# A fourth buffer for x, two fewer for the gate's projections, and half of the low parts of x made by VectorE, at the head of a hybrid encoder kernel

## The chip, the cores and the metric

The kernel runs on one core of a Trainium2 chip. The metric is the time of one execution on the device, in microseconds (us); the time of a kernel is the median of its runs. Engines are named as in the profile: PE (TensorE matmul; PEld its weight loads), DVE (VectorE), ACT (ScalarE), POOL (GpSimd), SP (SyncE, which issues all DMA transfers here; SPq is its queue).

## The reference

A trunk of two layers on 512 tokens of width 1024, all in f32. Layer 0 mixes tokens by neighbourhood attention, layer 1 by latent attention. Each layer ends with a gated addition of a "per-layer embedding" (PLE): a sigmoid gate times p[i] @ ple_w_proj[i]. The change touches only the head of layer 0.

```python
def rmsnorm(x, g):
    y = x * lax.rsqrt(jnp.mean(x * x, axis=-1, keepdims=True) + EPS)
    return y * g
...
for i in range(DEPTH):                                   # DEPTH = 2
    xn = rmsnorm(x, norm_g[i])
    y = mixer_na(xn, ...) if i % 2 == 0 else mixer_mla(xn, ...)   # x @ w_in -> q, k, v, z; attention; * silu(z); @ w_out
    h = x + y
    gate = jax.nn.sigmoid(rmsnorm(h, ple_norm[i]) @ ple_w_gate[i])
    x = h + gate * (p[i] @ ple_w_proj[i])
return rmsnorm(x, final_norm)
```

## The kernel before, in words

Every matrix product is done as three: each operand is cut into a high part (ACT copies it into the float32r type) and a low part, its "rest" (f32 value minus high part, made by POOL or DVE), and PE adds high x high, high x low and low x high in PSUM. So each weight tile that SP loads into `wraw` gives a `whi` (ACT, L76) and a `wlo` (POOL, L77), and `wraw`, `whi` and `wlo` have three buffers each.

A scheduler in the framework sets the order of the instructions of each engine from the code and from its own timeline; the order is then fixed, and each engine works through its list strictly in turn. A `tile_pool` hands out buffers by tag: a tile waits until the last readers of the tile that held its buffer are done.

The head of the program, `run` in the "pre" pool, goes as follows.

1. x comes in twice. `xT` is x with features on the partitions, 8 tiles of 128x512. Times the gain g0 it is cut into `rh` (ACT, L629) and `rl` (DVE, L630): the pair `raw`, x not yet normalised. The second form, `x` (L642), has tokens on the partitions, 4 tiles of 128x1024; ACT squares each in place and sums the squares into a column of `ssq` (L643).
2. `ple` makes p[0] @ ple_w_proj[0] for 4 token tiles and 2 column halves (n = 0, 1). The 8 results go from PSUM to tiles called `pe` (DVE for n = 0, L415; ACT for n = 1, L417), and from there SP stores them to DRAM (L418).
3. POOL turns `ssq` into 1/rms (L645, L646); PE transposes it, spread over 128 columns, into `ps_T` (L122), so that each column holds the factor of its token. ACT copies that to `R` (L649).
4. The gate's input z of the mixer is projected from `raw`, and scaled by R only afterwards (`z_phase`): z0 and z1 with weights loaded ahead (L167), then z2, z3 and z4 (L96; their results are `ps_S`, `ps_S` and `ps_mm`). DVE multiplies each by R (L159), ACT applies SiLU (L160).
5. For each of the 8 tiles of `xT`, DVE multiplies by ps_T and g0 (L653), ACT copies the high part `xh` (L654), POOL makes the rest `xl` (L655). This pair is x normalised.
6. `na_heads` follows, in the "na" pool. Its first product is v of head group 0, from xh and xl: 4 token tiles of 24 matmuls of 128x256 each (8 with xh and whi, 8 with xl and whi, 8 with xh and wlo). Then q and k of the first two heads, and attention.

In the rows of the engines' order that are quoted below, names carry the number of their buffer: `rh_125`, `rh_126`, `rl_127`, `rl_128` are the two halves of `raw`; `xh_129`, `xh_130`, `xl_131`, `xl_132` those of normalised x; `pe_82` to `pe_85` are the tensors in DRAM that hold PLE's results.

Of the kernel before, what the change touches and what calls it, by code (L numbers as in the profile page):

```python
# [13 lines left out]
F32 = mybir.dt.float32  # L14
F32R = mybir.dt.float32r
AF = mybir.ActivationFunctionType
ALU = mybir.AluOpType
AX = mybir.AxisListType
PSUM = bass.MemoryType.PSUM
P = 128  # L20
S = 512
D = 1024
NT = S // P
# [15 lines left out]
class Trunk:  # L39
# [567 lines left out]
    def run(self):  # L607
        tc, nc, a = self.tc, self.nc, self.a
        def pair(n):
            return [self.bigtile(f"{n}h{g}") for g in range(2)], [self.bigtile(f"{n}l{g}") for g in range(2)]  # L610
# [4 lines left out]
        with tc.tile_pool(name="pre", bufs=4, reuse_waits="tile") as pool:  # L615
            operands = self.ple_load(0, pool)
            g0 = pool.tile([P, KD], F32, name="g0", bufs=1)
            nc.sync.dma_start(g0, a["g0"])

            raw, xT = pair("r"), pair("x")  # L620
            part = lambda T, k: [T[s][k // 4][:, k % 4, :] for s in range(2)]
            xs = [pool.tile([P, S], F32, name="xT", tag="xT", bufs=8) for k in range(KD)]
            ws = [[self.wp.tile([P, 1024], d, name=n, tag=n, bufs=3)
                   for n, d in (("wraw", F32), ("whi", F32R), ("wlo", F32R))] for _ in range(2)]
            for h in range(2):
                for k in range(4 * h, 4 * h + 4):
                    nc.sync.dma_start(xs[k], a["xT"][k])
                    hi, lo = part(raw, k)
                    nc.scalar.activation(hi, xs[k], AF.Copy, scale=g0[:, k:k + 1])  # L629
                    nc.vector.scalar_tensor_tensor(lo, xs[k], g0[:, k:k + 1], hi.bitcast(F32), op0=ALU.mult,  # L630
                                                   op1=ALU.subtract)
                for j in range(2):
                    wr, hi, lo = (x[:, h * S:(h + 1) * S] for x in ws[j])
                    nc.sync.dma_start(wr, a["na_z"][j][:, h * S:(h + 1) * S])
                    nc.scalar.activation(hi, wr, AF.Copy)
                    nc.vector.tensor_tensor(out=lo, in0=wr, in1=hi.bitcast(F32), op=ALU.subtract)
            ws = [w[1:] for w in ws]
            nc.sync.dma_start(self.ident, a["ident"])
            ss = pool.tile([P, NT], F32, name="ssq", bufs=1)
            xt = [pool.tile([P, D], F32, name="x", tag="x", bufs=3) for t in range(NT)]  # L640
            for t in range(NT):
                nc.sync.dma_start(xt[t], a["x"][t])  # L642
                nc.scalar.activation(xt[t], xt[t], AF.Square, accum_out=ss[:, t:t + 1])  # L643
            self.ple(pool, 0, "pe", 8, operands)
            nc.gpsimd.tensor_scalar(ss, ss, 1.0 / D, EPS, op0=ALU.mult, op1=ALU.add)  # L645
            nc.gpsimd.tensor_tensor(out=ss, in0=ss, in1=self.half.to_broadcast([P, NT]), op=ALU.pow)  # L646
            turned = self.transposes([ss[:, t:t + 1].to_broadcast([P, P]) for t in range(NT)])
            R = pool.tile([P, S], F32, name="R", bufs=1)
            nc.scalar.activation(R, turned, AF.Copy)  # L649
            zs = self.z_phase(a["na_z"], raw, range(2), R=R, ws=ws)  # L650
            for k in range(KD):
                hi, lo = part(xT, k)
                nc.vector.scalar_tensor_tensor(xs[k], turned, g0[:, k:k + 1], xs[k], op0=ALU.mult, op1=ALU.mult)  # L653
                nc.scalar.activation(hi, xs[k], AF.Copy)  # L654
                nc.gpsimd.tensor_tensor(out=lo, in0=xs[k], in1=hi.bitcast(F32), op=ALU.subtract)  # L655
            zs.update(self.z_phase(a["na_z"], raw, range(2, 8 - NLATE), R=R))
        oT = ([self.bigtile(f"oh{g}") for g in range(2)], [self.bigtile(f"ol{g}") for g in range(2)])
        with tc.tile_pool(name="na", bufs=2, reuse_waits="tile") as pool:
# [176 lines left out]
```

## Time and profile before

| | before |
|---|---|
| median of 3 runs | 691.34 us (691.29 to 692.84) |
| profiled execution: its time | 689.97 us |
| profiled execution: its span | 688.2 us |
| mean granted PE clock | 0.992 of full |
| PE busy | 664.4 us (97%) |
| ACT busy | 406.6 us (59%) |
| POOL busy | 397.8 us (58%) |
| DVE busy | 363.8 us (53%) |
| HBM traffic, mean over the span | 109 GB/s |

The span is the time from the first to the last record of the profiled execution; its own time is 1.8 us longer. Busy shares are averages over all stages. In the rows of the timeline the first number is the start in us from the start of the span, the second the time from there to the end of the group, then the engine, the line, the operation, output and inputs with their shapes and the count; in brackets stands how long the engine was idle before, and what ended that.

### The profile page before, as it was taken

The numbers are of one execution on the slowest core, as the hardware profiler recorded it, in microseconds if no ns is written. First come the engines' busy times: TensorE is split into PE (matmuls) and PEld (weight loads), VectorE is DVE, ScalarE is ACT, GpSimd is POOL, SyncE is SP. The second block draws the span as 40 slices with busy tenths as digits, with TensorE's granted clock in tenths as the row PEclk, the third lists the DMA queues.
The fourth block names the chain that finished last, engine by engine and source line by source line (L and its number), as shares of the span: only waits on it lengthen the run. The fifth ranks groups of instructions, "written<-read, shape, count | busy, mean of one in ns | idle before, by whom it ended". The sixth has DMA issues, their size and how long they took to land.

```text
span 688.2 us, 10108 instructions
## 1 busy us (share of the span) xinstructions
PE 664.4 (97%) x3552; PEld 566.3 (82%) x3552; DVE 363.8 (53%) x829; ACT 406.6 (59%) x808; POOL 397.8 (58%) x312
## 2 busy tenths in 40 slices
PE   7988999999999999999999998999999999999995
PEld 5878898998988888788899886787888777888885
DVE  6140374637837614633524503788988886045334
ACT  6662576666767562643533634878888878426433
POOL 0385457466575565853044634777789867658511
PEclk9998999999999999999999999999999999999998
DMA  8932423323223128444242343203121201584222
GB/s 281 375 112 72 133 81 104 104 74 108 73 93 115 35 104 306 153 130 135 92 114 95 106 118 119 80 24 92 25 69 37 87 1 65 190 311 153 62 74 95
DMA packets 30371, 79.11 MB, mean 115 GB/s; under 512 B 3953, under 2 KB 7281, under 8 KB 30321
## 3 DMA queue, kind: packets, MB, share of 16 engines
q1 hardware_dynamic: 30320, 78.47, 34.5%
q8 instruction: 28, 0.46, 0.3%
q14 instruction: 23, 0.18, 0.1%
HBM read 66.92 MB, written 8.39 MB: 109 GB/s over the span
## 4 chain that ended last, share of the span: by engine, by line
PE 85%; ACT 6%; DVE 3%; POOL 2%; issue 2%; DMA 2%; SPq 0%; POOLq 0%; DVEq 0%; ACTq 0%
PE ps_mm L96 59%; PE ps_S L96 10%; PE ps_T L122 5%; PE ps_O L96 4%; PE ps_O L357 2%; PE ps_mm L167 2%; PE ps_T L345 1%; ACT ex L596 1%; DMA wraw<-proj 1%; ACT whi L76 1%; PE ps_S L310 1%; PE ps_S L309 1%; POOL xl L655 1%; DVE mx L594 1%; POOL wlo L77 1%
## 5 line engine op out<-in xcount | busy, mean ns | idle before, releaser
L77 POOL TENSOR_TENSOR wlo<-wraw,whi 128x1024 fp32r<-128x1024 f32 (+3 forms) x93 | 210.4, 2275 | 131.4 <-ACT whi L76 97.2
L76 ACT ACTIVATE whi<-wraw 128x1024 fp32r<-128x1024 f32 (+3 forms) x93 | 92.0, 999 | 83.8 <-PE ps_mm L96 20.2
L598 POOL TENSOR_TENSOR ex<-ex,rc 128x512 f32<-128x512 f32 x64 | 66.2, 1046 | 20.8 <-DVE rc L597 14.0
L96 PE MATMUL ps_mm<-whi,hnT 128*128 128x512 f32 (+1 forms) x272 | 69.7, 377 | 0.0
L96 PEld LDWEIGHTS ps_mm<-whi,hnT 128*128 128x128 f32 x272 | 49.5, 188 | 9.5
L332 POOL TENSOR_TENSOR ex<-ex,rc 128x128 f32<-128x128 f32 (+1 forms) x64 | 34.3, 560 | 37.9 <-DVE rc L328 36.4
L594 DVE TENSOR_REDUCE mx<-ps_S 128x1 f32<-128x512 f32 x64 | 43.7, 685 | 15.3 <-PE ps_S L96 14.3
L596 ACT ACTIVATE ex<-ps_S,mx 128x512 f32<-128x512 f32 x64 | 44.0, 689 | 8.2 <-DVE mx L594 6.7
L85 DVE TENSOR_TENSOR pt_lo<-ps_T,pt_hi 128x512 fp32r<-128x512 f32 x64 | 43.1, 679 | 5.0 <-ACT pt_hi L83 4.6
L327 ACT ACTIVATE ex<-ex,mx 128x128 f32<-128x128 f32 (+1 forms) x64 | 30.2, 473 | 21.9 <-DVE mx L323 21.5
L83 ACT ACTIVATE pt_hi<-ps_T 128x512 fp32r<-128x512 f32 x64 | 37.1, 598 | 7.6 <-PE ps_T L122 7.3
L96 PE MATMUL ps_mm<-xh,whi 128*128 128x512 f32 x152 | 41.0, 400 | 0.1
L96 PE MATMUL ps_mm<-wlo,hnT 128*128 128x512 f32 (+1 forms) x136 | 40.6, 379 | 0.0
L96 PE MATMUL ps_mm<-xh,wlo 128*128 128x512 f32 x152 | 39.2, 392 | 0.0
L96 PE MATMUL ps_mm<-xl,whi 128*128 128x512 f32 x152 | 38.8, 392 | 0.0
L122 PE MATMUL ps_T<-ident,ex 128*128 128x128 f32 x256 | 36.3, 273 | 0.2 <-DVE pt_lo L85 0.2
L122 PEld LDWEIGHTS ps_T<-ident,ex 128*128 128x128 f32 x256 | 30.7, 140 | 6.8 <-issue 0.7
L437 DVE TENSOR_TENSOR sg<-pe,sg 128x512 f32<-128x512 f32 (+1 forms) x17 | 12.5, 734 | 39.4 <-ACT sg L436 39.4
L96 PEld LDWEIGHTS ps_mm<-xl,whi 128*128 128x128 f32 x152 | 28.1, 188 | 5.8
L96 PEld LDWEIGHTS ps_mm<-xh,wlo 128*128 128x128 f32 x152 | 28.1, 188 | 5.5
L190 POOL TENSOR_TENSOR u<-u,z 128x512 f32<-128x512 f32 x16 | 20.6, 1290 | 19.6 <-DVE u L185 18.8
L106 POOL TENSOR_TENSOR rs<-ss,half 128x1 f32<-128x1 f32 x20 | 10.8, 549 | 36.2 <-DVE ss L105 34.9
(267 smaller groups left out, 1670.1 us busy)
## 6 DMA issues: line engine op xcount, KB each, us to landing
pe<-pe SPq DMA_DIRECT2D x32, 256.0 KB, 3.3
wraw<-na_qk SPq DMA_DIRECT2D x16, 512.0 KB, 3.4
wraw<-gate SPq DMA_DIRECT2D x16, 512.0 KB, 3.3
wraw<-na_v SPq DMA_DIRECT2D x8, 512.0 KB, 3.4
wraw<-na_o SPq DMA_DIRECT2D x8, 512.0 KB, 3.4
wraw<-mla_z SPq DMA_DIRECT2D x8, 512.0 KB, 3.7
wraw<-mla_o SPq DMA_DIRECT2D x8, 512.0 KB, 3.5
wraw<-na_z SPq DMA_DIRECT2D x6, 512.0 KB, 6.3
```

Source lines behind the costliest of these rows:

```text
L76: nc.scalar.activation(hi[:, c], raw[:, c], AF.Copy)
L77: (rest or nc.gpsimd).tensor_tensor(out=lo[:, c], in0=raw[:, c], in1=hi[:, c].bitcast(F32), op=ALU.subtract)
L83: nc.scalar.activation(hi, src, AF.Copy, scale=scale)
L85: nc.vector.tensor_tensor(out=lo, in0=src, in1=hi.bitcast(F32), op=ALU.subtract)
L96: last = nc.tensor.matmul(out, l, r, start=i == 0, stop=i == n - 1)
L122: self.nc.tensor.transpose(t[:, i * P:(i + 1) * P], b, self.ident)
L190: nc.gpsimd.tensor_tensor(out=u, in0=u, in1=z, op=ALU.mult)
L327: self.last_exp = nc.scalar.activation(e, e, AF.Exp, bias=mx[:, qt:qt + 1], accum_out=sm[:, qt:qt + 1])
L332: nc.gpsimd.tensor_tensor(out=e, in0=e, in1=rc[:, qt:qt + 1].to_broadcast([P, e.shape[1]]), op=ALU.mult)
L594: nc.vector.reduce_max(mx[:, c], sp, axis=AX.X, negate=True)
L596: nc.scalar.activation(ex, sp, AF.Exp, bias=mx[:, c], accum_out=sm[:, c])
L598: nc.gpsimd.tensor_tensor(out=ex, in0=ex, in1=rc[:, c].to_broadcast([P, S]), op=ALU.mult)
```

## The change

Three edits, all in `run`'s "pre" pool. The token-major `x` gets four buffers in place of three, so that none of its four tiles shares a buffer. The tag `pe` gets six buffers in place of eight, so that the last two of the eight PLE results reuse those of the first two. (4 KB per partition more for x, 2 x 2 KB less for pe.) And of the eight rests `xl` of normalised x, those with an even number are made by DVE, those with an odd number by POOL as before.

```diff
-            xt = [pool.tile([P, D], F32, name="x", tag="x", bufs=3) for t in range(NT)]
+            xt = [pool.tile([P, D], F32, name="x", tag="x", bufs=4) for t in range(NT)]
             for t in range(NT):
                 nc.sync.dma_start(xt[t], a["x"][t])
                 nc.scalar.activation(xt[t], xt[t], AF.Square, accum_out=ss[:, t:t + 1])
-            self.ple(pool, 0, "pe", 8, operands)
+            self.ple(pool, 0, "pe", 6, operands)
...
                 nc.scalar.activation(hi, xs[k], AF.Copy)
-                nc.gpsimd.tensor_tensor(out=lo, in0=xs[k], in1=hi.bitcast(F32), op=ALU.subtract)
+                (nc.vector, nc.gpsimd)[k % 2].tensor_tensor(out=lo, in0=xs[k], in1=hi.bitcast(F32), op=ALU.subtract)
```

The scheduler orders the head anew; behind the products of v every engine's order is as before, but for one weight load and three loads of the bias that change places on SP. Three places show it.

On SP, where all loads and stores are issued, in the stretch with the four tiles of x, the stores of PLE's results and the weights of z2, z3 and z4:

```order
-L642 DMA x<-x 128x1024 x3
+L642 DMA x<-x 128x1024 x4
 L418 DMA pe_82<-pe 128x512
 L418 DMA pe_83<-pe 128x512
 L418 DMA pe_84<-pe 128x512
 L418 DMA pe_85<-pe 128x512
-L75 DMA wraw<-na_z 128x1024 x2
-L642 DMA x<-x 128x1024
+L75 DMA wraw<-na_z 128x1024 x3
 L418 DMA pe_82<-pe 128x512
 L418 DMA pe_83<-pe 128x512
-L75 DMA wraw<-na_z 128x1024
```

The last tile of x moves ahead of the first four stores and of the weights of z2 and z3, and the weights of z4 ahead of two stores. On ACT the squares of the last two tiles of x likewise come ahead of the copies of the last two PLE results (the two that now reuse a buffer) and of the high parts of z2 and z3.

On PE, from the start of z2 (`ps_S`, first of its two) to the transposes of 1/rms near the end of z3, before:

```order
L96 MATMUL ps_S<-rh_125,whi 128x512 x4
L96 MATMUL ps_S<-rh_126,whi 128x512 x4
L96 MATMUL ps_S<-rl_127,whi 128x512 x4
L96 MATMUL ps_S<-rl_128,whi 128x512 x4
L96 MATMUL ps_S<-rh_125,whi 128x512 x4
L96 MATMUL ps_S<-rh_126,whi 128x512 x3
L96 MATMUL ps_S<-rh_125,wlo 128x512 x4
L96 MATMUL ps_S<-rh_126,wlo 128x512 x4
L96 MATMUL ps_S<-rh_126,whi 128x512
L96 MATMUL ps_S<-rl_127,whi 128x512 x4
L96 MATMUL ps_S<-rl_128,whi 128x512 x3
L122 MATMUL ps_T<-ident,ssq 128x128 x4
```

And now, from the end of z0 and z1 (L167) on:

```order
L167 MATMUL ps_mm<-rl_128,whi 128x512 x2
L167 MATMUL ps_mm<-rh_126,wlo 128x512 x2
L122 MATMUL ps_T<-ident,ssq 128x128 x4
L96 MATMUL ps_S<-rh_125,whi 128x512 x4
L96 MATMUL ps_S<-rh_126,whi 128x512 x4
L96 MATMUL ps_S<-rl_127,whi 128x512 x4
```

The four transposes move 39 matmuls forward, to the place right behind z0 and z1. No matmul is added or dropped. In the first tile of v the eight matmuls with xl and the eight with wlo now follow each other, where before those of the second tile were mixed in between.

On POOL, from its first work to the last rest of x:

```order
-L77 ISA
-L77 TENSOR_TENSOR wlo<-wraw,whi 128x1024 x2
+L645 ISA
 L645 TENSOR_SCALAR ssq<-ssq 128x4
 L646 TENSOR_TENSOR ssq<-ssq,half 128x4
 L77 TENSOR_TENSOR wlo<-wraw,whi 128x1024 x3
-L655 TENSOR_TENSOR xl_131<-xT,xh_129 128x512 x4
-L655 TENSOR_TENSOR xl_132<-xT,xh_130 128x512
+L655 TENSOR_TENSOR xl_131<-xT,xh_129 128x512 x2
 L77 TENSOR_TENSOR wlo<-wraw,whi 128x1024
-L655 TENSOR_TENSOR xl_132<-xT,xh_130 128x512 x3
+L655 TENSOR_TENSOR xl_132<-xT,xh_130 128x512 x2
+L77 TENSOR_TENSOR wlo<-wraw,whi 128x1024 x2
```

1/rms (L645, L646) moves ahead of the rests of z2 and z3, and the rests of x ahead of those of v's second weight tile and q's. On DVE the four rests that it takes over follow the eight products of L653, three of them ahead of z2's product with R, the fourth behind it.

## The prediction

> **What bounds the kernel now.** I read the page's busy shares first, then the busy time of the stages, then PE's timeline at its longest pause, and from there the engines that it waits for.
>
> ```profile
> PE 664.4 (97%) x3552; PEld 566.3 (82%) x3552; DVE 363.8 (53%) x829; ACT 406.6 (59%) x808; POOL 397.8 (58%) x312
> 45.57:64.87 19.30, 15.32 (x97) 13.93 (x96) 2.94 (x6) 5.71 (x12) 11.64 (x11) 0.82 0.18 62
> 64.87:688.20 623.33, 608.42 (x3286) 519.57 (x3284) 339.97 (x789) 370.07 (x751) 370.12 (x288) 1.00 0.32 104
> ```
>
> PE is the bound: other engines matter only where PE waits for them. The second row is the stage in which v is projected (duration, then busy time of PE, PEld, DVE, ACT, POOL, then PE's granted clock, DMA share and GB/s): PE has pauses in it and a clock of 0.82. Behind it, 623.33 us pass at full clock with 608.42 us of matmuls.
>
> PE's timeline, with an earlier pause for comparison:
>
> ```profile
> 12.31 0.50 PE L96 MATMUL ps_T<-whi 128*128 128x512 f32 x1 [0.42 <-ACT whi L399]
> ...
> 28.32 0.62 PE L167 MATMUL ps_mm<-rh,wlo 128*128 128x512 f32 x2
> 28.78 1.98 PE L96 MATMUL ps_S<-rh,whi 128*128 128x512 f32 x8
> ...
> 37.62 0.60 PE L122 MATMUL ps_T<-ident,ssq 128*128 128x128 f32 x4
> 37.97 0.48 PE L96 MATMUL ps_S<-rl,whi 128*128 128x512 f32 x1
> ...
> 45.57 2.25 PE L96 MATMUL ps_mm<-whi,xh 128*128 128x256 f32 x8
> 47.65 0.52 PE L96 MATMUL ps_mm<-whi,xl 128*128 128x256 f32 x3
> ...
> 52.74 0.79 PE L96 MATMUL ps_mm<-whi,xl 128*128 128x256 f32 x2 [2.77 <-POOL xl L655]
> 53.96 0.79 PE L96 MATMUL ps_mm<-whi,xl 128*128 128x256 f32 x2 [0.43 <-POOL xl L655]
> 55.19 0.58 PE L96 MATMUL ps_mm<-whi,xl 128*128 128x256 f32 x1 [0.43 <-POOL xl L655]
> ...
> 59.12 1.11 PE L96 MATMUL ps_mm<-whi,xh 128*128 128x256 f32 x8
> 60.07 1.12 PE L96 MATMUL ps_mm<-whi,xl 128*128 128x256 f32 x8
> ...
> 64.87 2.00 PE L96 MATMUL ps_mm<-xh,whi 128*128 128x512 f32 x8
> ```
>
> The stage holds 4 x 24 = 96 matmuls of 128x256. From 59.12 to 60.07 eight take 0.96 us (0.12 each), so 96 need 11.52 us; they take 64.87 - 45.57 = 19.30. The excess is 7.78 us: 3.63 in three pauses for POOL's `xl`, 2.08 - 0.96 = 1.12 in the first eight (45.57 to 47.65), the remaining 3.03 because matmuls run slowly after the pauses. The clock is lost by a pause of 2.77 us and its followers; the 0.42 us at 12.31 lost none.
>
> Why is `xl` late? POOL, DVE and ACT, in that order:
>
> ```profile
> 32.66 0.19 POOL L645 TENSOR_SCALAR ssq<-ssq 128x4 f32<-128x4 f32 x1
> 32.94 1.02 POOL L646 TENSOR_TENSOR ssq<-ssq,half 128x4 f32<-128x4 f32 x1
> 33.93 4.75 POOL L77 TENSOR_TENSOR wlo<-wraw,whi 128x1024 fp32r<-128x1024 f32 x2
> ...
> 49.12 2.34 POOL L77 TENSOR_TENSOR wlo<-wraw,whi 128x1024 fp32r<-128x1024 f32 x1
> 51.43 3.71 POOL L655 TENSOR_TENSOR xl<-xT,xh 128x512 fp32r<-128x512 f32 x3
> 38.88 1.29 DVE L159 TENSOR_TENSOR z<-ps_mm,R 128x512 f32<-128x512 f32 x2 [18.40 <-ACT R L649]
> 40.09 5.35 DVE L653 SCALAR_TENSOR_TENSOR xT<-ps_T,g,xT 128x512 f32<-128x512 f32 x8
> 45.36 1.28 DVE L159 TENSOR_TENSOR z<-ps_S,R 128x512 f32<-128x512 f32 x2
> 19.64 1.06 ACT L643 ACTIVATE x<-x 128x1024 f32<-128x1024 f32 x1 [0.83 <-DMA x<-x]
> 21.64 1.07 ACT L643 ACTIVATE x<-x 128x1024 f32<-128x1024 f32 x1
> 23.63 1.09 ACT L643 ACTIVATE x<-x 128x1024 f32<-128x1024 f32 x1
> 26.69 1.06 ACT L76 ACTIVATE whi<-wraw 128x1024 fp32r<-128x1024 f32 x1 [1.89 <-DMA wraw<-na_z]
> 28.01 1.06 ACT L76 ACTIVATE whi<-wraw 128x1024 fp32r<-128x1024 f32 x1 [0.26 <-DMA wraw<-na_z]
> 29.81 1.06 ACT L643 ACTIVATE x<-x 128x1024 f32<-128x1024 f32 x1 [0.74 <-DMA x<-x]
> 39.81 1.28 ACT L160 ACT_TABLE_LOAD   x1
> 42.17 2.70 ACT L654 ACTIVATE xh<-xT 128x512 fp32r<-128x512 f32 x5
> ```
>
> The fourth tile of x lands at 29.81, so 1/rms is done at 33.93, is transposed at 37.62, and DVE can normalise only from 40.09 to 45.36. POOL then makes eight rests of 1.24 us (3 in 3.71), with a weight rest in between, until 55.14. DVE has nothing to do meanwhile.
>
> **The change, part by part.**
>
> *Fourth buffer for x.* The weights of z2 and z3 land 26.69 and 28.01: 512 KB cost 1.32 us in the queue. The third tile had landed when ACT took it (23.63, no wait), so the fourth, now right behind it, lands by 24.95. ACT's squares follow at a pitch of 1.05 to 1.15, so the last ends at 26.1 at the latest, and POOL's two steps (32.66 to 33.93: 1.27) end by 27.4. PE comes to the transposes at 28.78: no wait, 1.4 us in hand. The transposes themselves cost 0.35 (37.62 to 37.97) in either place.
>
> What is moved back for it: z2's weights, by the 512 KB, to 28.01, their high part to 29.07. PE is through the transposes at 28.78 + 0.35 = 29.13, so this costs 0. If the fourth tile takes the 1.80 us it took between 28.01 and 29.81, the cost is 0.42; a gain is excluded, as PE doesn't wait there now.
>
> *Six buffers for PLE's results.* The last two copies on ACT wait for the first two stores, and the high parts of z2, z3 and z4 stand behind them on ACT.
>
> ```profile
> 16.15 2.38 SPq L418 DMA_DIRECT2D pe<-pe  x4
> DMA to landing us min/median/max: 7.2/7.6/8.2
> ```
>
> The second line is of the `pe` stores. Two issues start at 16.15 and about 16.75, land by 24.4 and 25.0, and with the fourth x ahead by 25.7 and 26.3; two copies of 0.58 end by 26.9. z2's weights land at 28.01 only: cost 0. The cover is 1.1 us; later stores would push PE one for one.
>
> *Normalising earlier.* z3's weights land at 29.33, their high part ends at 30.4, R at 30.95. DVE: two products with R (38.88 to 40.09: 1.21) to 32.2, eight of 0.66 to 37.4, 8.0 us earlier than now. ACT: z4's high part to 32.0, table load 1.28, two SiLU 1.06, four `xh` at 0.54 to 36.5, v's first high part to 37.5, four `xh` to 39.7, where PE needs them from 45.57. The 1.12 us of the first eight matmuls go.
>
> *Half of the rests on DVE.* Nearest rows for a DVE subtraction of 128x512 from two tiles in SBUF (count, then shortest, median and longest in ns; the first group beside an idle POOL, the second beside weight rests), and one stretch where both engines work:
>
> ```profile
> L400 DVE TENSOR_TENSOR wlo<-wraw,whi x7: 417/684/693, 4.2 to 14.8; 128x512 fp32r<-128x512 f32 x5, 128x256 fp32r<-128x256 f32 x2
> L677 DVE TENSOR_TENSOR hg<-r,gp x16: 681/1134/2898, 268.0 to 637.8; 128x512 f32<-128x512 f32 x16
> 281.63 4.07 DVE L677 TENSOR_TENSOR hg<-r,gp 128x512 f32<-128x512 f32 x2
> 275.21 9.93 POOL L77 TENSOR_TENSOR wlo<-wraw,whi 128x1024 fp32r<-128x1024 f32 x4 [3.90 <-ACT whi L76]
> ```
>
> One costs 0.66 alone and up to 2.9 beside POOL. I take turns: DVE waits for POOL's current instruction, runs, POOL goes on. POOL: three weight rests of 2.38 (33.93: 2 in 4.75) from 29.07 to 36.2, a rest of x to 37.45 and the next to 38.7; DVE's first to 39.35; v's first weight rest to 41.7; DVE's second to 42.4; POOL to 43.65; DVE's third to 44.3; POOL to 45.55; DVE's fourth to 46.2; v's second weight rest to 48.6; q's to 51.0. PE needs DVE's fourth at 45.57 + 0.96 + 0.48 + 0.24 = 47.25: in time. It needs v's second weight rest at 45.57 + 0.96 + 0.96 + 0.48 = 47.97: a new pause of 0.6. Without any waiting POOL ends that rest at 45.9, and the cost is 0; I take 0.6, since L677 is the same pair of engines and operands.
>
> [...]
>
> *After v.* q's weight rest is ready at 51.0, PE needs its high part at 45.57 + 11.52 + 0.6 = 57.7. The next weights' buffers come free by PE, so their work moves along. PE's longest waits behind 60 us are these:
>
> ```profile
> PE ps_S L96 <- ACT ex L596: 3.0, 4, 1.3
> PE ps_mm L96 <- ACT c L458: 0.8, 1, 0.8
> ```
>
> The whole list (8.2 us) names ACT and DVE, never a transfer, so nothing there stands still in absolute time: the gain is kept to the end.
>
> **Sum:** 7.78 - 0 - 0 - 0.6 = 7.2 us. The profiled execution (span 688.2, time 689.97) comes to 681.0 and 682.8. It ran 1.4 under the median of the runs, 691.34; against that I forecast 684.2.
>
> **The rivals.**
>
> 1. *POOL always wins.* If DVE's rests get in only where POOL pauses, behind q's weight rest at 48.3, four of 0.66 end at 51.0; PE pauses from 46.5 to 51.0 but for scraps, some 4 us, and loses the clock again (3.0). That returns 7 of 7.8: 690.5. Against it: at 275.21 POOL did four weight rests in 9.93, 0.4 more than 4 x 2.38, with DVE's two done in between at 281.63 to 285.70.
> 2. *The fourth tile still lands at 29.81.* Then 1/rms is ready at about 32.3, and PE, which now has the transposes ahead of z2, stands 3.5 us and loses the clock (3.0): 690.7. It decides from a landing after 26.3. For it: x took up to 8.8 us where others stood ahead; against it: now only three tiles do.
> 3. *Slower: ACT held by the stores.* If the first two stores land after 31.7, z2's high part comes after 33.3, PE's pause passes 4.2 us, and with the clock's 3.0 the gain is gone. At twice the longest time to land (16.75 + 16.4 + 1.3 = 34.5) it is a pause of 7.0: 691.34 - 7.2 + 10.0 = 694.1. Against it: the stores' narrow 7.2 to 8.2.
> 4. *Half-way.* One of DVE's rests loses a turn to a weight rest and comes 2 us late, with or without the clock: 686 to 689.
>
> [...]
>
> **How the numbers follow.** The forecast's case (682.5 to 686) gets 0.80, rival 4 0.10, rivals 1 and 2 together 0.06, rival 3 0.04. A measurement here can't tell less than 0.3% (2.1 us) from no change, so the first two are "faster" (0.90), the next "same", the last "slower". Low is the profiled execution less the whole excess, 689.97 - 7.78 = 682.2; high takes in most of rival 4, 688.0.
>
> **What would show it.** Right: the fourth square on ACT ends by 26.1; transposes at about 28.8 with no wait; DVE's products end at about 37.5; PE's v stage lasts 11.5 to 12.2 at a clock near 1.0, its only wait for POOL's `wlo`; every later stage as long as before. Wrong: a PE pause at 29, DVE's `xl` far over 1.5 us each, or v's stage over 14 us.

## The result, and the profile after

The changed kernel takes 682.95 us (median of 4 runs, 682.41 to 683.72), the kernel before 691.32 (689.97 to 692.84): 8.4 us less. The ratio is 0.9879, with a 95% interval of 0.9856 to 0.9902. The profiled execution of the changed kernel has a span of 680.6 us and a time of 682.41; before it was 688.2 and 689.97.

The two stages that the prediction speaks of, from the start of the transposes to v and from v to q (duration; busy time of PE, PEld, DVE, ACT, POOL; PE's clock; DMA share, GB/s):

```profile
29.03:45.82 16.79, 16.79 (x77) 13.96 (x76) 14.02 (x16) 12.72 (x19) 16.79 (x9) 1.00 0.55 192
45.82:57.34 11.52, 11.52 (x98) 11.51 (x97) 1.96 (x4) 3.58 (x7) 6.36 (x7) 1.00 0.42 144
```

v's stage lasts 11.52 us, just what 96 matmuls at 0.12 need, with PE busy throughout and at full clock; it was 19.30 at a clock of 0.82. The timeline of the changed kernel shows how that came about, ACT first, then POOL, DVE and PE:

```profile
23.66 1.05 ACT L643 ACTIVATE x<-x 128x1024 f32<-128x1024 f32 x1
25.81 0.59 ACT L417 COPY pe<-ps_O 128x512 f32<-128x512 f32 x1 [0.41 <-DMA pe<-pe]
27.88 1.06 ACT L76 ACTIVATE whi<-wraw 128x1024 fp32r<-128x1024 f32 x1 [1.48 <-DMA wraw<-na_z]
30.18 0.58 ACT L649 ACTIVATE R<-ps_T 128x512 f32<-128x512 f32 x1
25.16 1.02 POOL L646 TENSOR_TENSOR ssq<-ssq,half 128x4 f32<-128x4 f32 x1
36.14 3.00 POOL L655 TENSOR_TENSOR xl<-xT,xh 128x512 fp32r<-128x512 f32 x2
39.10 2.85 POOL L77 TENSOR_TENSOR wlo<-wraw,whi 128x1024 fp32r<-128x1024 f32 x1
41.91 3.45 POOL L655 TENSOR_TENSOR xl<-xT,xh 128x512 fp32r<-128x512 f32 x2
45.32 4.78 POOL L77 TENSOR_TENSOR wlo<-wraw,whi 128x1024 fp32r<-128x1024 f32 x2
32.00 5.35 DVE L653 SCALAR_TENSOR_TENSOR xT<-ps_T,g,xT 128x512 f32<-128x512 f32 x8
37.26 5.24 DVE L655 TENSOR_TENSOR xl<-xT,xh 128x512 fp32r<-128x512 f32 x3
43.02 1.18 DVE L655 TENSOR_TENSOR xl<-xT,xh 128x512 fp32r<-128x512 f32 x1
29.03 0.60 PE L122 MATMUL ps_T<-ident,ssq 128*128 128x128 f32 x4
29.39 2.09 PE L96 MATMUL ps_S<-rh,whi 128*128 128x512 f32 x8
...
45.82 1.11 PE L96 MATMUL ps_mm<-whi,xh 128*128 128x256 f32 x8
46.78 1.12 PE L96 MATMUL ps_mm<-whi,xl 128*128 128x256 f32 x8
...
57.34 2.00 PE L96 MATMUL ps_mm<-xh,whi 128*128 128x512 f32 x8
```

The fourth square starts at 23.66 (29.81 before), 1/rms is ready at 26.18 (33.93), DVE normalises from 32.00 (40.09), and the last rest of x is there at about 45.3 (55.14), before PE asks for the first at 46.78. From 29.03 to the start of q at 57.34 PE goes from matmul to matmul without a wait. Behind v, 680.6 - 57.34 = 623.26 us pass; before it was 623.33.

### The profile page after: what moved, and what is told of

Read it like the earlier page. It is cut to its first block, busy times and chain, and to the rows that moved or that the text cites. A ratio compares the mean times of both kernels' runs of the same rounds, so it can differ in the third digit from the quotient of the medians.

```text
span 680.6 us, 10112 instructions
## 1 busy us (share of the span) xinstructions
PE 660.7 (97%) x3552; PEld 564.2 (83%) x3552; DVE 369.4 (54%) x833; ACT 406.7 (60%) x808; POOL 395.2 (58%) x308
## 4 chain that ended last, share of the span: by engine, by line
PE 87%; ACT 5%; DVE 3%; issue 2%; DMA 1%; POOL 1%; SPq 0%; POOLq 0%; DVEq 0%; ACTq 0%
PE ps_mm L96 60%; PE ps_S L96 10%; PE ps_T L122 5%; PE ps_O L96 4%; PE ps_O L357 2%; PE ps_mm L167 2%; PE ps_T L345 1%; ACT ex L596 1%; ACT whi L76 1%; PE ps_S L310 1%; PE ps_S L309 1%; DVE mx L594 1%; PE ps_T L96 1%; DMA wraw<-pT 1%; DMA wraw<-mla_c 0%
## 5 line engine op out<-in xcount | busy, mean ns | idle before, releaser
L85 DVE TENSOR_TENSOR pt_lo<-ps_T,pt_hi 128x512 fp32r<-128x512 f32 x64 | 43.0, 679 | 5.0 <-ACT pt_hi L83 4.6
```

The lines of the kernel that those rows point to most:

```text
L85: nc.vector.tensor_tensor(out=lo, in0=src, in1=hi.bitcast(F32), op=ALU.subtract)
```

## The experiments

All times are against runs of the kernel before on the same chip. The v stage of each is read in its own profiled execution.

**Buffers alone** (four for x, six for PLE's results; POOL makes all rests):

```diff
-                (nc.vector, nc.gpsimd)[k % 2].tensor_tensor(out=lo, in0=xs[k], ...)
+                nc.gpsimd.tensor_tensor(out=lo, in0=xs[k], ...)
```

> The changed kernel with all eight rests of normalised x on POOL again: four x buffers and six for PLE's results are kept. Theory (the fourth x buffer carries the gain, by starting the normalising 8 us earlier): PE's transposes at about 29.0 without a wait, DVE's products from 32.0 to 37.3; POOL ends its eight rests at about 48.5 and v's second weight rest at about 51, PE pauses 0 to 1.5 us in v's stage and keeps its clock; the stage takes 11.5 to 13.0 us, the time is 682.9 to 684.5. Rival (the gain comes from the split, POOL being the bottleneck): v's stage takes 15 us or more, the time is 687 or more.

Measured: 683.66 us, ratio 0.9889 (0.9877 to 0.9902). The stage from v to q, POOL's rests and PE's one wait:

```profile
46.05:58.31 12.26, 11.80 (x98) 11.60 (x96) 1.97 (x4) 2.89 (x6) 9.09 (x8) 1.00 0.52 171
44.59 3.79 POOL L655 TENSOR_TENSOR xl<-xT,xh 128x512 fp32r<-128x512 f32 x3
48.34 4.72 POOL L77 TENSOR_TENSOR wlo<-wraw,whi 128x1024 fp32r<-128x1024 f32 x2
52.46 1.22 PE L96 MATMUL ps_mm<-whi,xh 128*128 128x256 f32 x8 [0.46 <-DVE vt L85]
```

POOL ends its last rest at 48.38 and v's second weight rest near 50.7, as expected. PE's one wait ends with DVE, which reads v's first results out of PSUM (L85). PE loses 12.26 - 11.52 = 0.74 us and keeps its clock. So the buffers carry nearly all of the gain, and the split is worth some 0.7 us on top of them. This 0.7 rests on the stage: the median is 0.71 above that of the changed kernel, and 0.5 and 0.6 above those of its variants with eight and four buffers, which ran on the same chip as this one, but the intervals overlap.

**Split alone** (three buffers for x, eight for PLE's results):

```diff
-                nc.gpsimd.tensor_tensor(out=lo, in0=xs[k], ...)
+                (nc.vector, nc.gpsimd)[k % 2].tensor_tensor(out=lo, in0=xs[k], ...)
```

> The kernel before with every other rest of normalised x on DVE, and three x buffers and eight for PLE's results as before. Theory (the fourth x buffer carries the gain): the fourth tile of x still lands at about 29.8, DVE's products stay at 40 to 45.4, the rests end at 51 to 54 and v's stage takes 16 to 18.5 us with PE's clock lost; the time is 688 to 690.5. Rival (the split carries the gain): v's stage takes 13 us or less, the time is under 686.

Measured: 689.81 us (12 runs), ratio 0.9983 (0.9971 to 0.9994). Its profiled execution was one of the long ones (691.84), with z2 at 30.53 and a v stage of 19.42, longer than the 16 to 18.5 that I expected. So it was run once more.

> The split alone once more, for a second look at its v stage: in its first profiled execution (691.84 us) the stage took 19.42 us and PE came to z2 at 30.53, while the median of its runs was 689.81. Theory (the split alone shortens PE's pauses, and the rest of the scatter lies in the first 29 us and in how long the clock stays lost): PE comes to z2 at 28.7 to 29.5, v's stage takes 16.5 to 19.4, time 689 to 690.5. Rival (the split alone leaves v's stage as it was, and the median's 1.8 us come from elsewhere): v's stage again 19.2 or more with the time at 690 or less.

Measured: 689.92 us in one run (the kernel before, one run on the same chip: 692.68); z2 at 28.84, v's stage from 45.63 to 64.84, 19.21 us:

```profile
46.62 5.62 DVE L655 TENSOR_TENSOR xl<-xT,xh 128x512 fp32r<-128x512 f32 x3
52.76 0.68 DVE L655 TENSOR_TENSOR xl<-xT,xh 128x512 fp32r<-128x512 f32 x1
48.94 0.51 PE L96 MATMUL ps_mm<-whi,xl 128*128 128x256 f32 x2 [1.06 <-DVE xl L655]
50.62 0.79 PE L96 MATMUL ps_mm<-whi,xl 128*128 128x256 f32 x2 [1.17 <-DVE xl L655]
52.29 0.80 PE L96 MATMUL ps_mm<-whi,xl 128*128 128x256 f32 x2 [0.88 <-DVE xl L655]
52.89 2.08 PE L96 MATMUL ps_mm<-whi,xh 128*128 128x256 f32 x8
```

The time lies in the ranges of both, and so does the stage: the theory's reached up to 19.4, the rival's began at 19.2. The stage is as good as unchanged. The four rests on DVE come behind two products of z and behind POOL's instructions, the last at 53.4 instead of 55.1. PE now waits for the very first rest (its first matmul with xl starts at 48.94; before, it started at 47.65 without a wait), and in place of pauses of 2.77, 0.43 and 0.43 us it makes three of about 1 us. The clock is lost all the same: the eight matmuls at 52.89 take 1.88 us to the next group, not 0.96. Which part of the median's 1.8 us gain is in this stage stays open: two profiled executions of each of the two kernels do not settle it.

**The kernel before once more**, for the scatter of its runs:

> The kernel before once more, for a second look at the scatter of its runs (689.86 to 692.91). Theory (the lost clock makes the scatter): PE's pauses for POOL's rests are the same to 0.2 us, the time that slow matmuls add differs; v's stage takes 18.5 to 21 us. Rival (the scatter lies in the first 29 us, with the loads): v's stage within 0.2 of 19.3, PE comes to z2 at another time than 28.78 by as much as the execution's time differs from 689.97.

Measured: 691.43 us, close to the median. PE comes to z2 at 29.30, 0.52 later than in the first profile, and v's stage lasts 20.10:

```profile
46.10 2.25 PE L96 MATMUL ps_mm<-whi,xh 128*128 128x256 f32 x8
...
53.28 0.51 PE L96 MATMUL ps_mm<-whi,xl 128*128 128x256 f32 x2 [2.78 <-POOL xl L655]
54.51 0.80 PE L96 MATMUL ps_mm<-whi,xl 128*128 128x256 f32 x2 [0.72 <-POOL xl L655]
55.74 0.58 PE L96 MATMUL ps_mm<-whi,xl 128*128 128x256 f32 x1 [0.43 <-POOL xl L655]
...
59.74 1.81 PE L96 MATMUL ps_mm<-whi,xh 128*128 128x256 f32 x8
...
66.20 2.00 PE L96 MATMUL ps_mm<-xh,whi 128*128 128x512 f32 x8
```

Both theories hold in part: 0.80 us of the 1.46 between the two executions lie in v's stage, 0.52 in the loads at the head. Within the stage all of the 0.80 comes behind the long pause: from its end to q it is 12.13 us in the first profile, 12.92 here. The clock was lost for equally long. Each trace grants PE half of its clock for 6.83 us on end (same columns as above; the first profile, then this one):

```profile
52.19:59.02 6.83, 5.42 (x22) 4.83 (x23) 0.43 (x1) 0.38 (x1) 5.02 (x7) 0.50 0.48 166
54.47:61.30 6.83, 6.36 (x28) 6.07 (x29) 0.85 (x2) 0.77 (x2) 3.29 (x5) 0.50 0.30 101
```

What differs is what falls into that time. In the first profile it begins 0.55 us before the long pause ends, and the two short pauses lie in it as well. Here it begins after the long pause, and PE works 6.36 us of it instead of 5.42. So the eight matmuls at 59.74 are slow here (1.65 us to the next group), while the same eight, at 59.12 in the first profile, ran at full speed (0.96). At half the clock the 0.94 us more of work cost 0.47 by my estimate; most of the rest is the second pause, 0.72 instead of 0.43.

**Eight buffers for PLE's results**, with the rest of the change kept:

```diff
-            self.ple(pool, 0, "pe", 6, operands)
+            self.ple(pool, 0, "pe", 8, operands)
```

> The changed kernel with eight buffers for PLE's results. Theory (the two lost buffers cost nothing, as ACT waits for z2's weights anyway): ACT's wait of 0.41 us for a store is gone, z2's high part starts at 27.9 as before, PE's rows are the same; time within 0.3% of the changed kernel, 682.4 to 684. Rival (the reuse delays ACT and PE behind it): 0.4 us or more faster than the changed kernel, 682.5 or less, with PE's transposes or z2 starting earlier.

Measured: 683.18 us, ratio 0.9883 (0.9869 to 0.9897); v's stage 11.52. ACT's wait for a store is gone, and z2's high part still starts only when its weights land, at 27.36. This interval and that of the changed kernel overlap, so the two buffers given up cost nothing that can be measured.

**Four buffers for PLE's results** (the same line, with 4):

> The changed kernel with four buffers for PLE's results, so that all four ACT copies wait for a store. Theory: the last of the first four stores lands at about 27.1, the last copy ends at about 27.7, z2's high part starts at 27.9 to 28.3, PE pauses 0 to 0.3 us ahead of z2; time 682.4 to 684.2. Rival (ACT held by the stores, the mechanism that could have made the change slower): the copies end after 29, PE stands 1 us or more at 29.4, time 685 or more.

Measured: 683.02 us, ratio 0.988 (0.9868 to 0.9893); v's stage 11.52.

```profile
25.81 0.59 ACT L417 COPY pe<-ps_T 128x512 f32<-128x512 f32 x1 [0.61 <-DMA pe<-pe]
26.29 0.59 ACT L417 COPY pe<-ps_O 128x512 f32<-128x512 f32 x1
27.15 1.06 ACT L76 ACTIVATE whi<-wraw 128x1024 fp32r<-128x1024 f32 x1 [0.26 <-DMA wraw<-na_z]
```

ACT waits longer for stores (0.26 and 0.61 us, against one wait of 0.41), but its copies still end at 26.88, before z2's weights land at 27.15. The stores that they need, issued ahead of the weights in the same queue, had landed by 26.29, where the last copy starts without a wait.

**Two buffers** (the same line, with 2). The framework reorders ACT, DVE, PE and SP for it: the high parts of z2 to z4 come ahead of PLE's copies on ACT, R behind them.

> The changed kernel with two buffers for PLE's results. The framework then puts R on ACT behind copies that wait for stores. Theory (the stores hold ACT once too few buffers are left): the last copies come at 33 or later, R at 34.5 to 37 (30.2 in the changed kernel), DVE's products start 4 to 6 us later, rests end at 47 to 51, PE pauses 0 to 3 us in v's stage; time 683.5 to 688. Rival (stores land early enough even so): R by 32, time as the changed kernel, 682.4 to 683.5.

Measured: 687.47 us, ratio 0.9944 (0.9924 to 0.9965).

```profile
34.77 0.59 ACT L417 COPY pe<-ps_O 128x512 f32<-128x512 f32 x1
36.29 0.60 ACT L649 ACTIVATE R<-ps_T 128x512 f32<-128x512 f32 x1 [0.93 <-PE ps_T L122]
48.63 0.50 PE L96 MATMUL ps_mm<-whi,xl 128*128 128x256 f32 x2 [0.94 <-DVE xl L655]
50.31 0.38 PE L96 MATMUL ps_mm<-whi,xl 128*128 128x256 f32 x1 [1.18 <-DVE xl L655]
46.10:62.29 16.19, 13.85 (x97) 13.19 (x96) 6.03 (x7) 3.47 (x8) 8.46 (x8) 0.89 0.24 71
```

Here the stores do set when the copies can be made: DVE waits 4.69 us for one (until 24.00), and on ACT, which has the high parts in between, the last copy starts at 34.77, right after the store that it needs landed at 34.70. R stands behind that copy and then waits 0.93 for PE's transposes, which the framework has moved back to 35.66. It comes 6.1 us later than in the changed kernel, two pauses of about 1 us follow in v's stage, the stage's mean clock is 0.89, and 16.19 - 11.52 = 4.67 us of the gain are gone. The cost is paid through R and the rests, and not, as the third rival of the prediction had it, through z2's weights.

**All rests on DVE:**

```diff
-                (nc.vector, nc.gpsimd)[k % 2].tensor_tensor(out=lo, in0=xs[k], ...)
+                nc.vector.tensor_tensor(out=lo, in0=xs[k], ...)
```

> The changed kernel with all eight rests of normalised x on DVE, none on POOL. Theory (DVE and POOL take turns at instructions that read two tiles of SBUF, as they did for the rests in the changed kernel): while POOL makes weight rests, a DVE rest takes up to 2.9 us, alone 0.66; the eight take 37.3 to 43 or 46, PE needs the last at 47.5 and doesn't pause: v's stage 11.5 to 12 us, time 682.4 to 684. Rival (the two engines don't hold each other up, DVE's rests were slow for another reason, such as waiting for ACT's high parts): eight rests take under 6 us from 37.3 although POOL works.

Measured: 683.15 us, ratio 0.988 (0.9861 to 0.9899); v's stage 11.52 with no wait.

```profile
37.64 3.09 DVE L655 TENSOR_TENSOR xl<-xT,xh 128x512 fp32r<-128x512 f32 x5
41.25 5.71 DVE L655 TENSOR_TENSOR xl<-xT,xh 128x512 fp32r<-128x512 f32 x3
38.60 7.21 POOL L77 TENSOR_TENSOR wlo<-wraw,whi 128x1024 fp32r<-128x1024 f32 x2 [2.06 <-ACT whi L76]
```

The eight rests take 9.3 us (I expected the end at 43 to 46; it was 46.96). Five of them follow each other at 0.6 each, although POOL's weight rest was issued at 38.60 in their midst: that one takes 4.40 us, and POOL's two together 7.21, which take 4.75 elsewhere. DVE's last three rests then take 5.71 us, the longest of them 2.88. So each engine held the other up here, but not in strict turns. In the changed kernel POOL got in after one rest of DVE (its rest that starts at 37.40 takes 1.74), here only after the fifth; why, these runs don't show. In this run with all rests on DVE, DVE's products (L653), which read one tile from PSUM and one from SBUF, kept to 0.66 each beside a busy POOL (eight in 5.36 us from 32.37), as they did at 32.00 in the changed kernel (eight in 5.35).

**The last x behind the stores:**

```diff
-            for t in range(NT):
+            for t in range(NT - 1):
                 nc.sync.dma_start(xt[t], a["x"][t])
                 nc.scalar.activation(xt[t], xt[t], AF.Square, accum_out=ss[:, t:t + 1])
             self.ple(pool, 0, "pe", 6, operands)
+            nc.sync.dma_start(xt[3], a["x"][3])
+            nc.scalar.activation(xt[3], xt[3], AF.Square, accum_out=ss[:, 3:4])
```

> The changed kernel with the load of the last tile of x issued behind the first four stores of PLE's results; the order on PE is as in the changed kernel, the transposes of 1/rms ahead of z2. Theory (1/rms has 2 to 3 us in hand before PE comes to the transposes): the tile lands 2.6 us later at about 26.2, its square ends at about 27.5, 1/rms at about 28.8, PE comes at 29.0 and waits 0 to 0.5 us; time 682.4 to 684.2. Rival (the transposes wait for every us of the load): PE stands 1.5 us or more ahead of them, time 685 or more.

Measured: 683.07 us, ratio 0.9877 (0.9859 to 0.9895); v's stage 11.52.

```profile
26.11 1.06 ACT L646 ACTIVATE x<-x 128x1024 f32<-128x1024 f32 x1 [1.59 <-DMA x<-x]
27.63 1.02 POOL L648 TENSOR_TENSOR ssq<-ssq,half 128x4 f32<-128x4 f32 x1
29.94 0.60 PE L122 MATMUL ps_T<-ident,ssq 128*128 128x128 f32 x4
```

1/rms is ready at 28.65 (2.47 us later than in the changed kernel), and PE doesn't wait. In this execution PE came to the transposes 0.9 later than in the changed kernel's, with the loads at the head; without that, 0.4 us would still be in hand.

**The last x loaded twice**, so that its square waits for the second load:

```diff
                 nc.sync.dma_start(xt[t], a["x"][t])
+                if t == 3:
+                    nc.sync.dma_start(xt[t], a["x"][t])
```

> The changed kernel with the last tile of x loaded twice into its buffer, so that its square waits for the second load; four x buffers, six for PLE's results and the split stay. The framework puts the transposes of 1/rms behind z3. Theory (what counts is when the last tile's data are there, not the buffers or the split in themselves): the second load lands at 30 to 33, the transposes come at about 39.5, DVE's products end at about 46.5, v's stage takes 15 to 19 us; time 687 to 691. Rival (the split or the other order of the loads carries the gain): v's stage under 13 us, time under 685.

Measured: 692.23 us (10 runs), ratio 1.0016 (1.0003 to 1.003): 1.2 us above the range expected.

```profile
32.79 1.06 ACT L645 ACTIVATE x<-x 128x1024 f32<-128x1024 f32 x1 [1.41 <-DMA x<-x]
39.61 0.60 PE L122 MATMUL ps_T<-ident,ssq 128*128 128x128 f32 x4
41.62 2.12 PE L96 MATMUL ps_mm<-rh,whi 128*128 128x512 f32 x8 [1.41 <-DVE z L159]
47.22:65.71 18.49, 15.20 (x98) 13.81 (x96) 9.05 (x11) 5.59 (x12) 7.80 (x7) 0.82 0.18 61
```

With all three edits in place but the data of the last tile there only at 32.79, the whole gain is gone: v's stage takes 18.49 us, and z4 waits another 1.41 for z0's product with R. What counts is when the last tile's data come in, with the place of the transposes that goes with it: the framework put them behind z3 here, and no run brings the data as late with the transposes left ahead of z2.

## Why the prediction was right

- **The fourth x.** Forecast: square done by 26.1, 1/rms by 27.4, PE at the transposes at 28.78 with no wait. Measured: square done at 24.8, 1/rms at 26.18, transposes at 29.03 with no wait (0.25 later, as the loads of this execution held z0 and z1 up). The slack is shown by the load moved behind the stores, and that the landing decides by the load made twice.
- **z2's weights moved back.** Forecast to land at 28.01, high part at 29.07, cost 0. Landed at 27.88, high part at 28.94, z2 at 29.39 right behind the transposes: cost 0.
- **Six buffers.** Forecast: copies end by 26.9, cost 0. They end at 26.40 after a wait of 0.41; eight and four buffers give the same time, two do not. The cover of 1.1 us was 1.48 in the trace.
- **Normalising earlier.** Forecast: DVE's products end at 37.4; measured 37.35. v's first eight matmuls take 46.78 - 45.82 = 0.96 us, so the 1.12 lost on them went too.
- **The rests by turns.** Here the term of 0.6 us was mis-sized: no pause came. I let each of DVE's four rests hold POOL up for a full 0.66, an estimate from the rows of L677. POOL's second weight rest of v started at 45.32 where four rests of 1.24 and one of 2.38 from 36.14 give 43.48: 1.84 for four, 0.46 each. The rest ended at about 47.7, PE asked for it at 45.82 + 2.40 = 48.22. In kind the turns were as told: DVE's first three rests take 0.72, 1.79 and 2.89 us while POOL works. That the two engines held each other up is borne out, though POOL lost 0.46 for each rest and not the 0.66 of a whole one. That they would take turns was my estimate, and on that the run with all rests on DVE differs: three of DVE's rests that began after POOL's instruction ran ahead of it.
- **After v.** Forecast: the gain is kept to the end. 623.26 against 623.33 us. (The waits of that list add up to 7.5 us, not 8.2; none of them is for a transfer.)
- **The sum.** 7.2 was forecast; the profiled executions differ by 7.6 in span, which is 7.78, less 0.25 at the head, plus 0.07 behind v. The medians differ by 8.4. The forecast gain was 1.2 too small: 0.6 for the pause that didn't come, and the rest, as far as one more profile shows, because the largest term was taken from one execution at the cheap end. The second profile of before, near the median, has a v stage of 20.10, an excess of 8.58 over the 11.52. Both errors went the same way, and 682.95 lies near the lower end of the range.
- **The rivals.** POOL never shut DVE out; the fourth tile landed in time; ACT's wait for stores stayed hidden; no rest came late, the last being there at 45.3. That a late tile, with late rests and a lost clock, eats such a gain is what the last x loaded twice shows, but by another path than in the second rival: the framework put the transposes behind z3, and PE paused in v's stage, not ahead of z2.

## What to carry to other kernels

Follow a wait of the bounding engine back to the first late event, not to the engine that happens to release it: POOL's rests ended PE's wait, and moving half of them away was worth 0.7 us with the input in time, and at most the 1.8 us of the medians without, of which v's stage shows nothing in two profiles, while one more buffer, which let a load start 5 us earlier, was worth eight. Buffers can be taken from where a wait is covered by a later one: here four instead of eight were free, since the stores stood ahead of the awaited weights in the same queue. Where a stage has pauses and a lost clock, take its excess from more than one execution.

## What the runs showed of the hardware that I had not expected

The clock was lost also in runs whose pauses were of about 1 us. With the split alone, in the second execution, PE paused for 1.06 us and then for 1.17, and the granted clock fell to half at 50.40, before the second pause was over and before the third (0.88). With two buffers the fall, at 51.59, came behind pauses of 0.94, 1.18 and 0.22, and the stage's clock was 0.89 on average. Neither stage had a longer pause; the kernel before had one of 2.77. One pause of 0.46 with the buffers alone cost none (1.00 in that stage). The length of one pause did not decide here: with the last x loaded twice, z4's wait of 1.41 us left the clock whole (1.00 from 28.70 to 47.22), and it fell at 50.37, in a pause of 1.26 behind eight matmuls that had themselves taken 2.02 us instead of 1.12.

Once lost, the clock stayed at half for one of two times here: 6.83 us in both executions of the kernel before, both of the split alone and that of the last x loaded twice, and 3.41 us, half as long, with two buffers. There PE had no pause in that time, in the other five it had; that this makes the difference is not shown. What the loss cost also differed with how much of PE's work fell into it: 5.42 us in one execution of the kernel before, 6.36 in the other.

The kernels without a lost clock also scattered less: the runs of the changed kernel and of the four variants with a v stage of 11.52 us lie between 682.41 and 684.14, those of before between 689.86 and 692.91, and the split alone between 689.08 and 692.56. That the lost clock makes this scatter is shown for 0.80 us of one difference only.
